# Where the last products of two unhalved tiles, one x cast and one bank copy stand in the first steps of a feed-forward

## The chip, the core and the metric

The kernel runs on one core of one Trainium2 chip. The metric is device time in microseconds of one execution, as the median of several runs. A profile of one execution gives the busy time of each engine: TensorE (PE for matmuls, PEld for weight loads), VectorE (DVE), ScalarE (ACT), GpSimd (POOL) and SyncE (SP, which here only issues DMAs).

## What is computed

A decoder trunk of two layers on 512 tokens of width 1024 in float32. Each layer is a half-step feed-forward, three token mixers side by side, and a second half-step feed-forward:

```python
def swiglu(h, w_in, w_out):
    gate, up = jnp.split(h @ w_in, 2, axis=-1)
    return (jax.nn.silu(gate) * up) @ w_out

for l in range(DEPTH):   # 2
    x = x + 0.5 * swiglu(rms_norm(x, ffn1_norm[l]), ffn1_w_in[l], ffn1_w_out[l])
    h = rms_norm(x, mix_norm[l]) @ w_mix_in[l]
    y = concatenate([short_conv(h), hgrn2(h), fox_attention(h)])   # pieces of h
    x = x + y @ w_mix_out[l]
    x = x + 0.5 * swiglu(rms_norm(x, ffn2_norm[l]), ffn2_w_in[l], ffn2_w_out[l])
```

The hidden width of a feed-forward is 2816, 22 tiles of 128 columns. The change touches the feed-forwards only, and of the four only the last three.

## The kernel before

**Numbers in two parts.** A float32 operand is split into a high part (a ScalarE cast to fp32r) and a low part (VectorE: the operand minus the high part). A product is then three matmuls, high x high (L312), high x low (L318) and low x high (L319), in `mm3`. So each operand costs ScalarE one pass and VectorE one pass before TensorE can use it.

**Tiles of a feed-forward.** The first hidden tiles, called covered (6 in the first feed-forward, 4 in the other three), are multiplied in full with the raw x while the norm is still being worked out; their banks are scaled by `self.inv` afterwards. `clear(f, i)` (L529 ff.) does this for one tile: two VectorE multiplications out of the banks into gi and ui, and a SiLU of gi on ScalarE (L266). `values(f, i)` then makes the hidden values gi * ui: two VectorE instructions of 128x256 (L673 and L670, "the last products" of that tile), written to the tiles hq. `values(0, 0)` and `values(0, 1)` belong to the first two covered tiles, (2, 0) and (2, 1) to the other two. The rest of the tiles go through `halved`, a Strassen-like scheme: a unit is a pair of hidden tiles (or of output tiles), and its product of 2x2 blocks is made with seven block products P1 to P7 instead of eight.

**A step.** `plan` writes down all steps of a feed-forward as a list. Step n is one block product of one unit, 24 matmuls of 128x256. The first unit's products come in the order P1, P2, P6, P5, P7, P3, P4 (steps 0 to 6), the next unit's P1 is step 7. In `halved` (loop at L843) a step issues, in this order: its 24 matmuls (`product`); `prepare` for the step three further on, that is, a ScalarE cast of its weights (L770) into one of three buffers hl, and later, as `rest()`, VectorE's subtraction for the low part (L772); between the two, what the product's own bank asks for; then the plan's extra work (`run(n)`: loads, sums of weight blocks, such as L758); and last the entry `self.entry[n]`, where there is one.

**Banks.** P1, P6, P7 and P4 of a unit share one PSUM bank and add to it; P2 has its own, P5 and P3 share a third. So a bank must be read before the next product writes to it: after P1 ScalarE copies it to g1 (L869); after P2 VectorE does g1 - bank (L872), and ScalarE the SiLU of it (L266); after P6 ScalarE copies the shared bank to g2 (L876); after P5 to u2 (L879); after P7 VectorE adds the shared bank to u2 (L882); after P3 to g2 (L885); after P4 the unit's hidden values are made (L673 and L670 with 128x512).

**The x of each product.** The seven products need seven sums of quarters of the normalised x. In the three later feed-forwards `enter` (from L545) makes them by hand: four quarters X (L580), then for P1, P2, P5 and P6 a high part (`high`, ScalarE, L593) and a low part (`lows[...]`, VectorE, L596 or L598) each, with additions between them (`add`, L603). Those of P7, P3 and P4 do not come before the loop of steps: they are issued at the end of steps 0 to 3, as functions in the dictionary `self.entry`, together with the last products of the covered tiles.

**What sets the order.** All these instructions of ScalarE, VectorE, POOL and SP are chained per engine by `follow` in the order in which the program issues them. So the order written in `enter`, `halved` and `self.entry` is the order on each engine, and an instruction that waits holds all behind it on that engine.

Of the kernel before, what the change touches and what calls it, by code (L numbers as in the profile page):

```python
# [13 lines left out]
AF = mybir.ActivationFunctionType  # L14
# [142 lines left out]
class Trunk:  # L157
# [381 lines left out]
    def values(self, fp, f, i, gi, ui, keep):  # L539
        V = (lambda i: self.follow("v", i)) if keep else (lambda i: i)  # L540
        a, k = divmod(f + i, 4)
        for b in range(2):
            V(self.hidden(self.quarter(fp, 0, a, b)[:, k, :], *(t[:, 256 * b : 256 * b + 256] for t in (gi, ui)), a != b))

    def enter(self, fp, w_in, then):  # L545
        nc = self.nc
        H = T // 2
        A, V = (lambda i, e=e: self.follow(e, i) for e in "av")

        def stream(f, banks, given):  # L550
            def parts(k, kk):
                r = slice(k * P, (k + kk) * P)
                return [w_in[r, f * P : (f + 2) * P], w_in[r, FF + f * P : FF + (f + 2) * P]]

            return self.stream_steps(
                [(bk, slice(c, c + P), None) for bk, c in zip(banks, (0, 256, 128, 384))],
                parts, self.xact, KD, given=given,
            )

        ba = self.next4()  # L560
        first = stream(0, ba, lambda k: k == KD - 2)
        for _ in range(4):
            next(first)
        nb = self.bank("pt" if self.ntog % 2 == 0 else "po")
        bb = self.next4()
        second = stream(2, bb, lambda k: True)
        self.ngain = self.const.tile([P, KD], F32, tag="ngain", name=self.n("ngain"))
        A(nc.scalar.activation(self.ngain, self.gain, AF.Copy, scale=-1.0))
        next(second)
        self.end_norm(nb, fp, True)  # L570
        self.table(SILU)
        next(first, None)
        next(then)
        X, self.xc, lows = {}, {}, {}

        def quarter(a, b):
            X[a, b] = t = fp.tile([P, 4, H], F32, tag=f"r{2 + 2 * a + b}", name=self.n("xn"))
            for k in range(4):
                i = 4 * a + k
                V(nc.vector.scalar_tensor_tensor(  # L580
                    out=t[:, k, :], in0=self.xT[:, i, b * H : (b + 1) * H],
                    scalar=(self.gain if a == b else self.ngain)[:, i : i + 1],
                    in1=self.inv[:, b * H : (b + 1) * H], op0=ALU.mult, op1=ALU.mult,
                ))

        def high(name):
            c = ORDER_IN.index(name)
            src, other = X[SUM[name]], name in NEGATIVE
            hi, lo = (
                fp.tile([P, 4, H], F32R, tag=f"x{w}{c}", name=self.n("xc")) for w in "hl"  # L590
            )
            self.xc[name] = hi, lo
            A(nc.scalar.activation(hi, src, AF.Copy, scale=-1.0) if other else nc.scalar.copy(hi, src))  # L593

            def low():
                V(nc.vector.scalar_tensor_tensor(  # L596
                    out=lo, in0=src, scalar=-1.0, in1=hi, op0=ALU.mult, op1=ALU.subtract
                ) if other else nc.vector.tensor_sub(lo, src, hi))  # L598

            lows[name] = low  # L600

        def add(x, y):
            V(nc.vector.tensor_add(X[x], X[x], X[y]))  # L603

        def both(name):
            high(name)
            lows[name]()

        def row():
            next(second)  # L610
            next(second, None)

        cleared = {}

        def clear(f, i):
            banks = bb if f else ba
            cleared[f, i] = self.clear(fp, banks[2 * i], banks[2 * i + 1], True)

        def values(f, i):
            self.values(fp, f, i, *cleared.pop((f, i)), True)  # L620

        quarter(0, 0)
        high("P1")
        quarter(1, 0)
        lows["P1"]()
        next(second)
        next(second)
        high("P2")
        quarter(0, 1)
        lows["P2"]()  # L630
        quarter(1, 1)
        next(second)
        next(second)
        add((0, 0), (0, 1))
        high("P5")
        clear(0, 0)
        lows["P5"]()
        next(second)
        next(second)
        next(second, None)  # L640
        add((0, 0), (1, 1))
        high("P6")
        self.given["total"]()
        lows["P6"]()
        self.given["prepare"](0)
        self.given["prepare"](1)
        clear(0, 1)
        add((0, 1), (1, 1))
        next(then)
        self.entry = {  # L650
            0: lambda: (high("P7"), values(0, 0), lows["P7"]()),
            1: lambda: (values(0, 1), high("P3")),
            2: lambda: (lows["P3"](), add((0, 0), (1, 0))),
            3: lambda: both("P4"),
            9: lambda: clear(2, 0),
            10: lambda: values(2, 0),
            12: lambda: clear(2, 1),
            13: lambda: values(2, 1),
        }
# [66 lines left out]
    def halved(self, fp, w_in, w_out, covered):  # L726
        nc = self.nc
# [3 lines left out]
        A, V, G, S = (lambda i, e=e: self.follow(e, i) for e in "avgs")  # L731
# [13 lines left out]
        def add(u, q, q2):  # L745
            G(nc.gpsimd.dma_start(raw[u, q], src(u, q2), accum_op=ALU.add))
# [70 lines left out]
        u = seq[0][:2]  # L817
# [25 lines left out]
        for n, (kind, w, p) in enumerate(seq):  # L843
# [3 lines left out]
            if p in new:  # L847
# [3 lines left out]
                u, p, acc, p in new, p in ("P2", "P3", "P4"),  # L851
                kind == "I" and p == "P1" and w in (covered, *(f0 for f0, _ in CHUNKS)),
            )
            rest = prepare(*seq[n + LEAD]) if n + LEAD < len(seq) else None
            if kind == "O":
                c, g = w

                for r, b, f in {
                    "P2": ((0, 0, -0.5),), "P1": ((0, 0, -0.5),), "P5": ((1, 1, -0.5),),
                    "P6": ((0, 1, -0.5),), "P7": ((1, 1, 0.5),), "P3": ((0, 1, 0.5),),  # L860
                    "P4": ((1, 0, 0.5),),
                }[p]:
                    xs = self.xT[:, 4 * r + 2 * g : 4 * r + 2 * g + 2, b * H : (b + 1) * H]
                    V(nc.vector.scalar_tensor_tensor(
                        out=xs, in0=pair(acc), scalar=f, in1=xs, op0=ALU.mult, op1=ALU.add
                    ))
            elif p == "P1":
                work[u, "g1"] = g1 = tmp("g1")
                A(nc.scalar.activation(g1, acc, AF.Copy, scale=-1.0))  # L869
            elif p == "P2":  # L870
                g1 = work[u, "g1"]
                V(nc.vector.tensor_sub(g1, g1, acc))  # L872
                A(self.act(g1, g1, AF.Silu))
            elif p == "P6":
                work[u, "g2"] = g2 = tmp("g2")
                A(nc.scalar.activation(g2, acc, AF.Copy, scale=-1.0))  # L876
            elif p == "P5":
                work[u, "u2"] = u2 = tmp("u2")
                A(nc.scalar.activation(u2, acc, AF.Copy, scale=-1.0))  # L879
            elif p == "P7":  # L880
                u2 = work[u, "u2"]
                V(nc.vector.tensor_add(u2, u2, acc))  # L882
            elif p == "P3":
                g2 = work[u, "g2"]
                V(nc.vector.tensor_add(g2, g2, acc))  # L885
                A(self.act(g2, g2, AF.Silu))
            else:
                g1, g2, u2 = (work[u, x] for x in ("g1", "g2", "u2"))
                c = next(i for i, (f0, nf) in enumerate(CHUNKS) if f0 <= w < f0 + nf)
                if c < 2:  # L890
                    a, k = divmod(w - CHUNKS[c][0], 4)
                    for b, g, v in ((1, g2, u2), (0, g1, acc)):
                        V(self.hidden(
                            self.quarter(fp, c, a, b)[:, k : k + 2, :], pair(g), pair(v), a != b
                        ))
                else:
                    q = (w - CHUNKS[c][0]) // 2
                    y = fp.tile([P, 2, T], F32, tag="S", name=self.n("y"), bufs=2)
                    V(nc.vector.tensor_mul(y[:, :, H:], pair(g2), pair(u2)))
                    V(nc.vector.tensor_mul(y[:, :, :H], pair(g1), pair(acc)))  # L900
                    hh, hl = (
                        fp.tile([P, 2, T], F32R, tag=f"r{t}", name=self.n("hh")) for t in tags[q]
                    )
                    self.hh.append(hh)
                    self.hl.append(hl)
# [746 lines left out]
```

## Time and profile before

| what | value |
|---|---|
| runs | 1847.47 us median of 3 (1844.77 to 1851.09) |
| the profiled execution | 1844.32 us |
| its span, first to last instruction | 1842.5 us |
| granted TensorE clock, mean over the span | 1.000 of full speed |
| instructions | 34734 |
| entries (first steps of the halved tiles) | from about 640, 967 and 1547 us |

Times inside the profile are microseconds from the start of the span. A row of the timeline gives the start, the duration, the engine, the line of the kernel, the operation with the tiles that it writes and reads, and in brackets how long the engine stood idle before it and what ended that. A row of the waits gives the engine and line that waited, what it waited for, the total in microseconds, how often, and the longest. Durations of neighbouring instructions overlap a little, so the distance from start to start says what an instruction costs its engine. Ends of matmuls are modelled, so for TensorE too the starts are the better measure.

### The profile page before, as it was taken

The numbers are of one execution on the slowest core, as the hardware profiler recorded it, in microseconds if no ns is written. First come the engines' busy times: TensorE is split into PE (matmuls) and PEld (weight loads), VectorE is DVE, ScalarE is ACT, GpSimd is POOL, SyncE is SP. The second block draws the span as 40 slices with busy tenths as digits, with TensorE's granted clock in tenths as the row PEclk, the third lists the DMA queues.
The fourth block names the chain that finished last, engine by engine and source line by source line (L and its number), as shares of the span: only waits on it lengthen the run. The fifth ranks groups of instructions, "written<-read, shape, count | busy, mean of one in ns | idle before, by whom it ended". The sixth has DMA issues, their size and how long they took to land.

```text
span 1842.5 us, 34734 instructions
## 1 busy us (share of the span) xinstructions
PE 1817.2 (99%) x14328; PEld 1686.7 (92%) x14328; DVE 1459.7 (79%) x2007; ACT 991.1 (54%) x1403; POOL 169.1 (9%) x168
## 2 busy tenths in 40 slices
PE   8999999999999999999999999999999999999999
PEld 6899999899877899999889999988997778999997
DVE  7888887676797898879678887966849878887883
ACT  4455555454676465555445555545547655555552
POOL 0011120100000001112001111201000000020210
PEclk9999999999999999999999999999999999999999
DMA  7659684233323767868265787823233237677762
GB/s 206 169 115 198 173 176 99 74 84 82 86 75 98 213 135 161 196 161 165 82 204 128 169 190 179 172 63 82 71 86 81 81 107 203 160 153 191 149 138 91
DMA packets 244782, 250.94 MB, mean 136 GB/s; under 512 B 19440, under 2 KB 229872, under 8 KB 244624
## 3 DMA queue, kind: packets, MB, share of 16 engines
q1 hardware_dynamic: 191024, 182.64, 33.0%
q0 software_dynamic: 53600, 66.09, 22.4%
q8 instruction: 112, 1.84, 0.4%
q14 instruction: 46, 0.38, 0.1%
HBM read 223.98 MB, written 2.10 MB: 123 GB/s over the span
## 4 chain that ended last, share of the span: by engine, by line
PE 87%; DVE 6%; ACT 3%; issue 2%; DMA 1%; SPq 0%; ACTq 0%
PE mm L312 13%; PE mm L319 12%; PE mm L318 12%; PE sc L312 6%; PE sc L319 6%; PE sc L318 6%; PE pt L312 6%; PE pt L318 6%; PE pt L319 6%; PE po L312 4%; PE po L318 4%; PE po L319 3%; DVE hl L302 1%; DVE hl L772 1%; PE po L1504 1%
## 5 line engine op out<-in xcount | busy, mean ns | idle before, releaser
L770 ACT CAST hl<-w 128x1024 fp32r<-128x1024 f32 x322 | 337.1, 1049 | 319.2 <-PE mm L319 77.7
L772 DVE TENSOR_TENSOR hl<-w,hl 128x1024 fp32r<-128x1024 f32 x322 | 392.6, 1221 | 92.3 <-ACT hl L770 92.0
L302 DVE TENSOR_TENSOR hl<-st,hl 128x512 fp32r<-128x512 f32 (+2 forms) x196 | 166.4, 851 | 121.0 <-ACT hl L301 119.5
L301 ACT CAST hl<-st 128x512 fp32r<-128x512 f32 (+2 forms) x196 | 146.5, 749 | 208.0 <-PE po L319 81.7
L312 PE MATMUL mm<-xc,hl 128*128 128x256 f32 (+1 forms) x732 | 201.7, 276 | 1.8 <-ACT g L876 1.4
L319 PE MATMUL mm<-xc,hl 128*128 128x256 f32 x728 | 201.4, 277 | 0.0
L318 PE MATMUL mm<-xc,hl 128*128 128x256 f32 x728 | 201.3, 277 | 0.0
L312 PE MATMUL sc<-xc,hl 128*128 128x256 f32 (+1 forms) x530 | 146.8, 278 | 2.5 <-ACT g L876 1.7
L319 PE MATMUL sc<-xc,hl 128*128 128x256 f32 x528 | 146.6, 278 | 0.0
L318 PE MATMUL sc<-xc,hl 128*128 128x256 f32 x528 | 146.4, 277 | 0.0
L312 PEld LDWEIGHTS mm<-xc,hl 128*128 128x128 f32 x732 | 137.3, 188 | 2.5 <-ACT g L876 1.8
L318 PEld LDWEIGHTS mm<-xc,hl 128*128 128x128 f32 x728 | 136.8, 188 | 0.0
L319 PEld LDWEIGHTS mm<-xc,hl 128*128 128x128 f32 x728 | 136.7, 188 | 0.1
L312 PE MATMUL pt<-xc,hl 128*128 128x256 f32 (+1 forms) x484 | 133.4, 277 | 0.0
L318 PE MATMUL pt<-xc,hl 128*128 128x256 f32 x480 | 133.2, 278 | 0.0
L319 PE MATMUL pt<-xc,hl 128*128 128x256 f32 x480 | 133.0, 277 | 0.0
L312 PE MATMUL mm<-x,hl 128*128 128x512 f32 x272 | 108.9, 401 | 0.7 <-ACT cy L1152 0.7
L319 PE MATMUL mm<-x,hl 128*128 128x512 f32 x272 | 107.6, 396 | 0.0
L318 PE MATMUL mm<-x,hl 128*128 128x512 f32 x272 | 106.7, 392 | 0.0
L312 PEld LDWEIGHTS sc<-xc,hl 128*128 128x128 f32 x530 | 99.5, 188 | 3.3 <-ACT g L876 2.1
L319 PEld LDWEIGHTS sc<-xc,hl 128*128 128x128 f32 x528 | 99.6, 189 | 0.1
L318 PEld LDWEIGHTS sc<-xc,hl 128*128 128x128 f32 x528 | 99.2, 188 | 0.0
(483 smaller groups left out, 5611.3 us busy)
## 6 DMA issues: line engine op xcount, KB each, us to landing
w<-in_ffn_w_in_dram SPq DMA_DIRECT2D x140, 512.0 KB
w<-in_ffn_w_out_dram SPq DMA_DIRECT2D x64, 512.0 KB
w<-in_ffn_w_out_dram POOLq DMA_DIRECT2D x56, 512.0 KB, 9.3
st<-in_w_mix_in_dram SPq DMA_DIRECT2D x88, 256.0 KB
st<-in_ffn_w_in_dram SPq DMA_DIRECT2D x72, 256.0 KB
w<-in_ffn_w_in_dram POOLq DMA_DIRECT2D x35, 512.0 KB, 8.3
w<-S POOLq DMA_DIRECT2D x35, 512.0 KB, 4.8
st<-in_ffn_w_out_dram SPq DMA_DIRECT2D x24, 512.0 KB
```

What stands on the lines that cost most here:

```text
L301: a = nc.scalar.copy(hi, src[:, c : c + w])
L302: b = nc.vector.tensor_sub(lo, src[:, c : c + w], hi)
L312: i = nc.tensor.matmul(acc[:, c], ah, bh[:, c], start=first and c.start == 0, stop=False, skip_group_check=True,)
L318: nc.tensor.matmul(acc, ah, bl, start=False, stop=False, skip_group_check=True)
L319: i = nc.tensor.matmul(acc, al, bh, start=False, stop=last, skip_group_check=True)
L770: A(nc.scalar.copy(hi, src))
L772: return lambda: V(nc.vector.tensor_sub(lo, src, hi))
L1504: nc.tensor.matmul(self.ob[:, t0 + u * P : t0 + 2 * P], V[:, j, h % 4].rearrange("p a d -> p (a d)"), part[:, j, u:, :].rearrange("p i t - ...
```

## The change

In `enter`, the last products of the covered tile (0, 0) move from the end of step 0 to a place ahead of the loop, and those of (0, 1) from step 1 to the end of step 7. P3's low x moves from step 2 to step 1, behind its high x, and the addition that makes P4's operand moves with it. In `halved`, for the first unit of the three feed-forwards that have an entry, ScalarE's copy of P6's bank to g2 is issued ahead of the weight cast of that step instead of behind it.

```diff
         clear(0, 1)
         add((0, 1), (1, 1))
         next(then)
+        values(0, 0)
         self.entry = {
-            0: lambda: (high("P7"), values(0, 0), lows["P7"]()),
-            1: lambda: (values(0, 1), high("P3")),
-            2: lambda: (lows["P3"](), add((0, 0), (1, 0))),
+            0: lambda: both("P7"),
+            1: lambda: (both("P3"), add((0, 0), (1, 0))),
             3: lambda: both("P4"),
+            7: lambda: values(0, 1),
             9: lambda: clear(2, 0),
...
                 kind == "I" and p == "P1" and w in (covered, *(f0 for f0, _ in CHUNKS)),
             )
+            if kind == "I" and p == "P6" and self.entry and w == covered:
+                work[u, "g2"] = g2 = tmp("g2")
+                A(nc.scalar.activation(g2, acc, AF.Copy, scale=-1.0))
             rest = prepare(*seq[n + LEAD]) if n + LEAD < len(seq) else None
...
                 A(self.act(g1, g1, AF.Silu))
+            elif p == "P6" and (u, "g2") in work:
+                pass
             elif p == "P6":
                 work[u, "g2"] = g2 = tmp("g2")
                 A(nc.scalar.activation(g2, acc, AF.Copy, scale=-1.0))
```

## The prediction, made before the changed kernel ran

> **What bounds the kernel now.** I read the page's first part, then the whole-span list of waits for TensorE, then the timeline of one entry engine by engine (634 to 690 us), and last the same stretch of the other two entries.
>
> ```profile
> PE 1817.2 (99%) x14328; PEld 1686.7 (92%) x14328; DVE 1459.7 (79%) x2007; ACT 991.1 (54%) x1403; POOL 169.1 (9%) x168
> ```
> ```profile
> PE sc L312 <- ACT g L876: 1.7, 2, 0.9
> ...
> PE mm L312 <- ACT g L876: 1.4, 2, 0.9
> ...
> PE sc L312 <- DVE u L882: 0.7, 2, 0.4
> ...
> PE mm L312 <- DVE u L882: 0.4, 1, 0.4
> ```
>
> TensorE is the bound: busy 99% of the span. So a change gains only where TensorE itself stands still. Two waits bear on this change: L876, the ScalarE copy of P6's bank into g2, and L882, the VectorE add that reads P7's bank. Entry 1 (the feed-forward at 640 us) shows where they fall. Each row below but the third is the first matmul of a product: P5, P7 (then P7's second matmul), P3, P4, and the next unit's P1 and P2.
>
> ```profile
> 648.15 0.28 PE L312 MATMUL pt<-xc,hl 128*128 128x256 f32 x1
> ...
> 651.90 0.39 PE L312 MATMUL sc<-xc,hl 128*128 128x256 f32 x1 [0.87 <-ACT g L876]
> ...
> 652.12 0.28 PE L318 MATMUL sc<-xc,hl 128*128 128x256 f32 x1
> ...
> 654.74 0.28 PE L312 MATMUL pt<-xc,hl 128*128 128x256 f32 x1
> ...
> 657.98 0.36 PE L312 MATMUL sc<-xc,hl 128*128 128x256 f32 x1 [0.36 <-DVE u L882]
> ...
> 660.80 0.28 PE L312 MATMUL pt<-xc,hl 128*128 128x256 f32 x1
> ...
> 663.52 0.28 PE L312 MATMUL sc<-xc,hl 128*128 128x256 f32 x1
> ```
>
> An undisturbed product takes 663.52 - 660.80 = 2.72 us for its 24 matmuls. The four from P5 on took 3.75, 2.84, 3.24 and 2.82. Their excess is 1.03 + 0.12 + 0.52 + 0.10 = **1.77 us** per entry: more than the 0.87 + 0.36 that the waits name, because the idle counts begin at a modelled matmul end, and because the first matmul after each stall goes slower (652.12 - 651.90 = 0.22, where 2.72/24 is 0.113). The other two entries show the same two stalls:
>
> ```profile
> 979.13 0.39 PE L312 MATMUL mm<-xc,hl 128*128 128x256 f32 x1 [0.87 <-ACT g L876]
> ...
> 985.22 0.36 PE L312 MATMUL mm<-xc,hl 128*128 128x256 f32 x1 [0.36 <-DVE u L882]
> ```
> ```profile
> 1558.80 0.39 PE L312 MATMUL sc<-xc,hl 128*128 128x256 f32 x1 [0.86 <-ACT g L876]
> ...
> 1564.88 0.36 PE L312 MATMUL sc<-xc,hl 128*128 128x256 f32 x1 [0.36 <-DVE u L882]
> ```
>
> So the most that can come from this is 3 x 1.77 = **5.3 us**, 0.29% of the span; about 0.3% is what a measurement of this kernel can tell from no change.
>
> The Trainium skill, "TensorE: Matmul & The Clock Gate", Part 1, "Wait — 56ns, not 53.3ns?", gives a warm matmul N / 2.4 GHz plus some 2.5 ns. An estimate from that page is 109 ns at N = 256, or 2.62 us per product, so an excess of 12.65 - 4 x 2.62 = 2.17 us per entry and 6.5 us in all. The trace differs: undisturbed products beside the stalls take 2.72 us, so the 5.3 stands.
>
> **Why TensorE waits there.** ScalarE and VectorE in that stretch of entry 1, in their order:
>
> ```profile
> 648.84 0.64 ACT L266 ACTIVATE g<-g 128x512 f32<-128x512 f32 x1 [1.27 <-DVE g L872]
> 649.38 1.03 ACT L593 CAST xc<-xn 128x1024 fp32r<-128x1024 f32 x1
> 650.32 1.04 ACT L770 CAST hl<-w 128x1024 fp32r<-128x1024 f32 x1
> 651.26 0.58 ACT L876 ACTIVATE g<-sc 128x512 f32<-128x512 f32 x1
> 651.75 1.04 ACT L770 CAST hl<-w 128x1024 fp32r<-128x1024 f32 x1
> ...
> 654.92 1.06 ACT L593 ACTIVATE xc<-xn 128x1024 fp32r<-128x1024 f32 x1 [1.63 <-DVE xn L603]
> ```
> ```profile
> 646.32 0.42 DVE L673 TENSOR_TENSOR hq<-gi,ui 128x256 f32<-128x256 f32 x1
> 646.65 0.42 DVE L670 SCALAR_TENSOR_TENSOR hq<-gi,ui 128x256 f32<-128x256 f32 x1
> 646.99 1.22 DVE L596 SCALAR_TENSOR_TENSOR xc<-xn,xc 128x1024 fp32r<-128x1024 f32 x1
> 648.12 0.68 DVE L872 TENSOR_TENSOR g<-g,sc 128x512 f32<-128x512 f32 x1
> 648.72 1.22 DVE L772 TENSOR_TENSOR hl<-w,hl 128x1024 fp32r<-128x1024 f32 x1
> 649.86 0.42 DVE L673 TENSOR_TENSOR hq<-gi,ui 128x256 f32<-128x256 f32 x1
> ...
> 651.39 1.22 DVE L772 TENSOR_TENSOR hl<-w,hl 128x1024 fp32r<-128x1024 f32 x1 [0.78 <-ACT hl L770]
> 652.53 1.22 DVE L598 TENSOR_TENSOR xc<-xn,xc 128x1024 fp32r<-128x1024 f32 x1
> 653.66 1.22 DVE L603 TENSOR_TENSOR xn<-xn,xn 128x1024 f32<-128x1024 f32 x1
> 654.80 1.22 DVE L772 TENSOR_TENSOR hl<-w,hl 128x1024 fp32r<-128x1024 f32 x1
> 656.01 1.23 DVE L596 SCALAR_TENSOR_TENSOR xc<-xn,xc 128x1024 fp32r<-128x1024 f32 x1
> 657.16 0.68 DVE L882 TENSOR_TENSOR u<-u,sc 128x512 f32<-128x512 f32 x1
> ```
>
> VectorE's add at 648.12 reads P2's bank, free since P6 began at 648.15 - 2.72 = 645.43, so it comes 2.7 us late, held by VectorE's own list. ScalarE's SiLU waits for it, then come P3's x, a weight cast, and only then P6's copy, which ends at 651.84; P7 starts 0.06 later. The add for P7's bank stands at the end of an unbroken VectorE run from 651.39, ends at 657.84, and P4 starts 0.14 later.
>
> **The change, part by part.** In each entry three things move on VectorE and one on ScalarE; the order of TensorE, POOL and SP is the same, and so is every DMA issue. No instruction is added or removed.
>
> 1. The pair (0,0) of last products, two VectorE instructions costing 646.99 - 646.32 = 0.67 us, goes ahead of the loop: in front of the low half of the third weight product. That slot is free, as VectorE next stands idle for 1.62 us (row at 644.04 below). The low half ended at 644.04 - 1.62 = 642.42, now 643.1 at the latest, and is first needed by P6 at 645.43, so the price is nothing; without that idle it would be 0.67 per entry. From 646.32 on VectorE runs 0.67 earlier: P7's low x ends at 647.5, the add L872 starts at 647.45, the SiLU at 648.17, P3's high x at 648.71.
> 2. P6's copy passes one cast, worth 650.32 -> 651.26 = 0.94 us. It starts at 648.71 + 0.94 = 649.65 and ends at 650.24 (P6's product is complete: P5 began at 648.15). P7's turn is 648.15 + 2.72 = 650.87: the copy is 0.6 ahead, and the **first stall goes**. The passed cast starts at 650.14, after 650.32 before, so it does not get later; its weight tile comes by a POOL transfer issued at 638.9 that landed within 6.5 us (rows below).
> 3. The pair (0,1) leaves VectorE's list ahead of the casts' subtractions, and P3's low x and the following add move ahead of the subtraction for P3's weights. P3's low x can start when ScalarE has its high half, 648.71 + 1.03 + 0.03 = 649.77; behind it, at 1.14 to 1.2 each as in the rows from 651.39, come the add (650.9), the two subtractions (652.05, 653.2), P4's low x (654.4) and the add L882 (655.55 to 656.23). This is 1.6 earlier than 657.16. ScalarE's share, P4's high x, waits for the add: in the row at 654.92 it starts 0.04 after the add's 653.66 + 1.22; now it may from 652.2 on, behind a cast and a bank copy, and is done ahead of 654.4. P4 can start at 656.23 + 0.14 = 656.37; its turn is 648.15 + 3 x 2.72 = 656.31. So the **second stall shrinks to about 0.06**, with perhaps 0.1 for a slower first matmul.
> 4. New wait: P3 now waits by itself for its weights' low half, which ends at 653.3; the matmul that reads it is due at 653.59 + 0.23. Cover 0.5 us, price nothing; if it failed, P3 and all behind it would be late by the shortfall.
> 5. The pair (0,1) is added at step 7, ahead of the next unit's L872 add. Behind that wait the SiLU, a cast and the next copy. VectorE's idle there:
>
> ```profile
> 644.04 1.23 DVE L772 TENSOR_TENSOR hl<-w,hl 128x1024 fp32r<-128x1024 f32 x1 [1.62 <-ACT hl L770]
> ...
> 668.41 1.23 DVE L772 TENSOR_TENSOR hl<-w,hl 128x1024 fp32r<-128x1024 f32 x1 [0.60 <-ACT hl L770]
> 670.29 1.23 DVE L772 TENSOR_TENSOR hl<-w,hl 128x1024 fp32r<-128x1024 f32 x1 [0.66 <-ACT hl L770]
> ```
> ```profile
> L787 POOL DMA_DIRECT2D w<-S x1: 887/887/887, 638.9 to 638.9; - x1
> ...
> DMA to landing us min/median/max: 6.5/6.5/6.5
> ```
> ```profile
> 670.16 0.59 ACT L876 ACTIVATE g<-pt 128x512 f32<-128x512 f32 x1
> ```
>
> The 0.67 is nearly all taken by the 0.60 of idle right behind, and the copy of the next unit ended at 670.75, 0.9 before its P7 at 660.80 + 4 x 2.72 = 671.68. Price nothing; uncovered, at most 0.67 per entry.
>
> **Sum.** Entries 1 and 3 gain 1.77 - 0.15 = 1.6 each; entry 2, whose second stall has the same size, 1.6 to 1.77. Together 5.0 us, between 0 (nothing reaches the end) and 5.3. Nearer 5.3 than 0, since the list of waits names no TensorE wait in later halved steps of these three feed-forwards (the rest of the 1.4 above belongs to the first one, which the change leaves alone). The profiled run took 1844.32 us, 1.8 more than its span of 1842.5, and goes to 1839.3. The median of the three runs shown is 1847.47, 3.15 above the profiled run; from it the forecast is **1842.4**.
>
> **Rivals.**
> - *The second stall stays in part.* If ScalarE's SiLU chain comes d later than worked out, P4 waits d longer, since VectorE's five following instructions have no gap. With d = 0.8, about the idle 0.78 that VectorE had at 651.39, an entry gains 1.6 - 0.8 = 0.8, together 2.4: 1845.1. For it: only 0.06 separates P4's turn from the add. Against it: the order of ScalarE ahead of that point is unchanged.
> - *VectorE is the limit, or a transfer takes the gain back.* Nothing is removed, so work that only moves gives nothing where VectorE has no idle: 1847.5. The Trainium skill, "VectorE: DVE Perf Modes", section "Rules for kernel authors", says to cut the number of instructions, since each pays its flush however they are chained; by it the moved pairs cost the same wherever they stand. Against it: the idle of 1.62, 0.60 and 0.66 us above. For the transfers: weights loaded long before would not come earlier with TensorE.
> - *The pair at step 7 costs more than it frees.* The next unit's L872 comes 0.67 late, its copy passes the 0.9 of slack, and P7 of that unit stalls as the first unit's did, at 1.15 us (1.03 + 0.12), while L882 of the first unit keeps its old time and P4's start with it. Then nothing is gained and 3 x 1.15 = 3.5 is lost: 1851.0, slower. It decides once VectorE's queue at step 8 is over 0.9 us later against TensorE than in these rows; the idle rows speak against it.
>
> **How the numbers follow.** Forecast 0.75, second stall in part 0.12, swallowed 0.08, slower 0.05. The bound of 0.3% is 5.5 us, so faster means under 1841.9. The three runs of before lie 6.3 us apart, so a median near 1842.4 falls on either side: I give the forecast 0.5 faster, 0.48 same, 0.02 slower; the partial case 0.15, 0.8, 0.05; the swallowed one 0.05, 0.8, 0.15; the last 0, 0.3, 0.7. Faster 0.40, same 0.54, slower 0.06. The range goes from the 5.3 with the lower runs' scatter (1838) to the swallowed gain (1847).
>
> **What would show it.** Right: in the profile after, the list of waits has no TensorE wait for the g2 copy at the three entries and at most a trace of L882, four products from P5 on take 10.9 to 11.1 us instead of 12.65, and P6's copy ends before 650.9 by this clock. Wrong: a new TensorE wait at P3 (its low half), or at the next unit's P7; or the stalls gone while the span is unchanged, which would mean that a transfer or a later stage took it.

## The result

| | before | after |
|---|---|---|
| median of 7 runs, us | 1845.43 (1841.21 to 1851.09) | 1838.22 (1835.24 to 1839.66) |
| ratio | | 0.9961, 95% interval 0.9945 to 0.9977 |
| profiled execution, us | 1844.32 | 1837.37 |
| its span, us | 1842.5 | 1835.6 |

The changed kernel is 0.39% faster, 7.2 us by the medians. The forecast from the median of three runs was 1842.4, that is, 5.0 us less; the time lies inside the range by 0.2 us. Two more measurements of the same two kernels gave 0.9966 (0.9952 to 0.9979) and 0.9971 (0.9955 to 0.9987).

First the list of TensorE's waits over the whole span of the profile after (engine, line, what it waited for, total, times, longest), from its third row to the row for the copy:

```profile
PE pt L1551 <- DVE KB L1473: 1.6, 6, 0.3
PE pt L1245 <- issue: 1.4, 1, 1.4
PE sc L1307 <- issue: 1.3, 2, 0.7
PE po L312 <- DVE nt L399: 1.3, 1, 1.3
PE mm L312 <- ACT cy L1158: 0.8, 2, 0.4
PE po L1510 <- ACT PH L1553: 0.6, 2, 0.3
PE mm L312 <- ACT g L882: 0.5, 1, 0.5
```

L882 is the old place of P6's copy in the new numbering; its one wait of 0.5 belongs to the first feed-forward. The copy's other waits are gone: neither its new place (L857) nor the add for P7's bank (now L888) has a row in the list. The same products as before, P5, P7, P3, P4, then the next unit's P1 and P2, in the timeline of entry 1:

```profile
647.90 0.28 PE L312 MATMUL pt<-xc,hl 128*128 128x256 f32 x1
...
650.62 0.28 PE L312 MATMUL sc<-xc,hl 128*128 128x256 f32 x1
...
653.34 0.28 PE L312 MATMUL pt<-xc,hl 128*128 128x256 f32 x1
...
656.07 0.33 PE L312 MATMUL sc<-xc,hl 128*128 128x256 f32 x1
...
658.83 0.28 PE L312 MATMUL pt<-xc,hl 128*128 128x256 f32 x1
...
661.55 0.28 PE L312 MATMUL sc<-xc,hl 128*128 128x256 f32 x1
```

They take 2.72, 2.72, 2.73 and 2.76: 10.93 in place of 12.65. What is left of the two stalls is 0.05 us. ScalarE and VectorE in that stretch of the same timeline:

```profile
647.91 0.63 ACT L266 ACTIVATE g<-g 128x512 f32<-128x512 f32 x1 [0.60 <-DVE g L876]
648.45 1.04 ACT L593 CAST xc<-xn 128x1024 fp32r<-128x1024 f32 x1
649.40 0.58 ACT L857 ACTIVATE g<-sc 128x512 f32<-128x512 f32 x1
649.88 2.04 ACT L771 CAST hl<-w 128x1024 fp32r<-128x1024 f32 x2
```
```profile
647.20 0.68 DVE L876 TENSOR_TENSOR g<-g,sc 128x512 f32<-128x512 f32 x1
647.80 1.22 DVE L773 TENSOR_TENSOR hl<-w,hl 128x1024 fp32r<-128x1024 f32 x1
649.53 1.23 DVE L598 TENSOR_TENSOR xc<-xn,xc 128x1024 fp32r<-128x1024 f32 x1 [0.51 <-ACT xc L593]
650.67 1.22 DVE L603 TENSOR_TENSOR xn<-xn,xn 128x1024 f32<-128x1024 f32 x1
651.80 2.35 DVE L773 TENSOR_TENSOR hl<-w,hl 128x1024 fp32r<-128x1024 f32 x2
654.07 1.22 DVE L596 SCALAR_TENSOR_TENSOR xc<-xn,xc 128x1024 fp32r<-128x1024 f32 x1
655.21 0.68 DVE L888 TENSOR_TENSOR u<-u,sc 128x512 f32<-128x512 f32 x1
```

This execution reached the entry 0.25 us earlier than the one of before (first product at 639.61; in before at 639.86). With that taken off, the prediction's times are met almost to the hundredth: the copy (L857) ends at 649.98 where 649.99 was worked out, P3's low x (L598) starts at 649.53 for 649.52, the add L888 ends at 655.89 for 655.98, and P4 starts at 656.07 for 656.12.

**Where the 6.9 us between the two spans came from.** I cut both spans at points that both have: the norms (the first matmul of L405), and the products whose first matmul is split in two (the first of each chunk of hidden tiles; in the timeline a row with 128x128 and x2). The differences, after minus before, in order:

| stretch | before, us | after, us | difference |
|---|---|---|---|
| start of the span to entry 1 | | | -0.25 |
| entry 1 to the next chunk | 40.0 | 38.3 | -1.7 |
| the chunk behind it | 114.5 | 118.9 | +4.4 |
| entry 2 to the next chunk | 40.8 | 39.1 | -1.7 |
| mixer of layer 2, norm to norm | 259.8 | 258.2 | -1.6 |
| entry 3 to the next chunk | 40.0 | 38.3 | -1.7 |
| the chunk behind it | 118.9 | 114.6 | -4.3 |
| the rest | | | -0.1 |

The three entries give 5.1 (the expectations below have it as 5.2). The two chunks trade places: one of them takes 118.9 us for the same matmuls in either profile, the second feed-forward's in one, the fourth's in the other. The mixer of layer 2, which no instruction of the change touches, gave 1.6. So theory A says: the change gains the 5.1 of the entries, and the rest is scatter of single executions. Theory B: it also took something away outside the entries. A second question is how the parts act together: each its own share, or in series.

### The profile page after: what moved, and what is told of

Same layout as the page of the kernel before. It is cut to its first block, busy times and chain, and to the rows that moved or that the text cites. A ratio compares the mean times of both kernels' runs of the same rounds, so it can differ in the third digit from the quotient of the medians.

```text
span 1835.6 us, 34734 instructions
## 1 busy us (share of the span) xinstructions
PE 1815.1 (99%) x14328; PEld 1685.2 (92%) x14328; DVE 1459.1 (79%) x2007; ACT 991.8 (54%) x1403; POOL 169.1 (9%) x168
## 4 chain that ended last, share of the span: by engine, by line
PE 89%; DVE 5%; ACT 3%; issue 1%; DMA 1%; SPq 1%; ACTq 0%
PE mm L312 13%; PE mm L319 13%; PE mm L318 13%; PE sc L319 6%; PE sc L318 6%; PE sc L312 6%; PE pt L312 6%; PE pt L318 6%; PE pt L319 6%; PE po L312 4%; PE po L318 4%; PE po L319 4%; DVE hl L302 1%; PE po L1510 1%; ACT hl L301 1%
```

## The experiments

All ratios are against the kernel before, run on the same chip in the same series; the comparisons of one series share its runs of before. The ratios differ from the quotients of the two medians by up to 0.0008, which is 1.5 us.

### The same two kernels again

No edit.

> The kernel before, once more, against itself. Both theories: ratio 1.000 with an interval of some 0.002 each way. Theory A (the change gains what the two stalls cost, 5.2 us, and the other 1.7 us of the difference of the two profiled spans, 6.9, is scatter): the excess of the four products from P5 on over 4 x 2.72 us is again about 1.77 us in entries 1 and 3, and places other than the entries differ from the first profile of before by a microsecond or more, among them the stretches of some 100 us in which a product takes 2.83 instead of 2.72 us. Theory B (the change also took something away outside the entries): outside the entries this profile agrees with the first one of before to a few tenths.

> The changed kernel once more. Theory A: 5.2 us less than before, ratio 0.9972; the excess of the four products from P5 on is below 0.1 us in each entry; the layer-2 mixer, where the first profile of after was 1.5 us shorter than that of before, is not shorter by the same amount again. Theory B: ratio 0.9961 or less again, and the mixer again 1.5 us shorter.

> The changed kernel a third time, on another day's scatter. Theory A (the gain is what the stalls cost): 5.2 us less than before, ratio 0.9972, entries of 38.3 us (39.1 where the slow pace sets in). Rival (the change also keeps TensorE out of slow stretches): ratio 0.9964 or less again.

Before against itself: 0.9999 (0.9987 to 1.0011). After: 0.9966 (0.9952 to 0.9979), and 0.9971 (0.9955 to 0.9987) the third time. Entries to the next chunk, in us: before 40.0, 40.8, 40.8; after 39.1, 39.1, 38.3 and 38.3, 38.3, 38.3. An entry that has 0.8 more than its kernel's shortest has it as slow pace, not as a wait: its products behind P4 take 2.83 instead of 2.72. In the first entry of the second profile of after that pace begins with P4 itself, so the excess there is 0.16 and not below 0.1, as was expected. The mixer of layer 2 took 261.2 in the repeat of before, and 260.2 and 262.8 in those of after, 258.2 to 262.8 in all profiles, with the longest of them in the changed kernel. So theory B's loss there did not come back. The ratios of after, 0.9961 to 0.9971, agree with theory A's 0.9972, each interval holding it; but all three lie below it, and a gain of some microseconds more (by the lower ends up to 3), everywhere and evenly, they cannot exclude.

### The copy alone

```diff
+            if kind == "I" and p == "P6" and self.entry and w == covered:
+                work[u, "g2"] = g2 = tmp("g2")
+                A(nc.scalar.activation(g2, acc, AF.Copy, scale=-1.0))
             rest = prepare(*seq[n + LEAD]) if n + LEAD < len(seq) else None
```
(against the kernel before; self.entry as there. The branch for P6 further down then passes, as in the change.)

> Only P6's bank copy ahead of the cast; the entries as before. Theory A: the first stall nearly goes (copy ends at 650.9 by the clock of before, P7 due 650.87), but the cast behind the copy comes 0.49 us later, and with it VectorE's unbroken run up to the add for P7's bank, so P4 starts at about 658.5 instead of 657.98: 0.5 us more per entry, 1.5 us slower in all, ratio 1.0008. Rival (each part gives its own share of the gain, the copy the first stall of 1.15 us): 3.4 us faster, ratio 0.998.

Measured 0.9995 (0.9986 to 1.0005). The timeline of entry 1 (which began 2.5 us later in this execution; P5 at 650.66), with P7, P3, P3's second matmul, P4 and the next unit's P1, then VectorE's add:

```profile
653.46 0.39 PE L312 MATMUL sc<-xc,hl 128*128 128x256 f32 x1
...
656.39 0.28 PE L312 MATMUL pt<-xc,hl 128*128 128x256 f32 x1
656.79 0.39 PE L318 MATMUL pt<-xc,hl 128*128 128x256 f32 x1
...
660.97 0.36 PE L312 MATMUL sc<-xc,hl 128*128 128x256 f32 x1 [1.28 <-ACT hl L770]
...
663.78 0.28 PE L312 MATMUL pt<-xc,hl 128*128 128x256 f32 x1
```
```profile
654.37 1.23 DVE L772 TENSOR_TENSOR hl<-w,hl 128x1024 fp32r<-128x1024 f32 x1 [1.26 <-ACT hl L770]
...
660.14 0.68 DVE L887 TENSOR_TENSOR u<-u,sc 128x512 f32<-128x512 f32 x1
```

The first stall shrinks from 1.03 to 0.08 (653.46 - 650.66 = 2.80). A new one comes at P3, whose second matmul starts 0.40 behind its first instead of 0.11. P4 starts 10.31 us after P5 instead of 9.83: the 0.5 worked out, and the four products take 13.12 in place of 12.65. So the copy alone makes the entry worse, by 0.47: VectorE's subtraction waits 1.26 (0.78 before) for the cast that was passed, and its unbroken run ends 0.47 later. The rival of shares asked for 3.4 us off, ratio 0.998; the profile refutes it, and the interval does not reach so low. The time does not show the 1.4 us: its interval ends at 1.0005, a little under the 1.0008 expected. And one lesson in reading: the row at 660.97 blames a ScalarE cast, yet P4 needs no cast that late; the add that it does need ended at 660.14 + 0.68 = 660.82, 0.15 ahead of it, as 0.14 before the change.

### The moves in the entries alone

```diff
+        values(0, 0)
         self.entry = {
-            0: lambda: (high("P7"), values(0, 0), lows["P7"]()),
-            1: lambda: (values(0, 1), high("P3")),
-            2: lambda: (lows["P3"](), add((0, 0), (1, 0))),
+            0: lambda: both("P7"),
+            1: lambda: (both("P3"), add((0, 0), (1, 0))),
             3: lambda: both("P4"),
+            7: lambda: values(0, 1),
```
(against the kernel before; the copy behind the cast as there)

> Only the moves in the entries; P6's copy stays behind the cast. Theory A: ScalarE runs 0.67 us earlier, the copy ends at about 651.2 by the clock of before, P7 is late by 0.35 and some 0.1 for its slow first matmul; P4 does not wait. An entry gains 1.77 - 0.45 = 1.3, together 3.9 us, ratio 0.9979. Rival (shares that add up: the copy the first stall, the entry moves the second): 1.9 us faster, ratio 0.999, with P7 still late by 0.8 or more.

> The entry moves without the copy, once more: its first runs lay 5.9 us under before, where its stalls in the profile account for 3.9. Theory A with scatter: 3.9 us, ratio 0.9979, entries of 38.7, 38.7 to 39.8 and 38.7 us. Rival (the entry moves also keep TensorE out of the stretches in which a product takes 2.83 us): again 6 us or more, ratio 0.9967 or less, and no stretch of 118.9 us between two chunks.

Measured 0.9962 (0.9949 to 0.9976) and 0.9983 (0.9962 to 1.0004). In the timeline of entry 1, P6's copy, and P7, which was due 2.72 after P5 at 648.38:

```profile
650.83 0.58 ACT L877 ACTIVATE g<-sc 128x512 f32<-128x512 f32 x1
```
```profile
651.46 0.39 PE L312 MATMUL sc<-xc,hl 128*128 128x256 f32 x1 [0.20 <-ACT g L877]
```

P7 is late by 0.36 and P4 not at all; the four products take 659.75 - 648.38 = 11.37. That is 1.28 off an entry, as expected; 38.7 us to the next chunk. The first series measured more than the 3.8 us that this makes, the second about that, and the second's profile has a chunk of 118.9 us: the moves do not keep the slow pace away.

### The first pair alone, and with the copy

```diff
+        values(0, 0)
         self.entry = {
-            0: lambda: (high("P7"), values(0, 0), lows["P7"]()),
+            0: lambda: both("P7"),
             1: lambda: (values(0, 1), high("P3")),
```
(against the kernel before; second kernel: this and the copy ahead of the cast)

> Only the pair (0,0) goes ahead of the loop; the pair (0,1) stays ahead of P3's subtraction, P3's low x stays at step 2, the copy stays behind the cast. Theory A: ScalarE runs 0.67 us earlier, so P7 is late by 0.35 and 0.1 for its slow first matmul; VectorE's unbroken run starts 0.67 earlier, so P4 starts at 657.3 by the clock of before instead of 657.98. Each entry gains 0.66, from the entry's first product to the next chunk's 39.3 us instead of 40.0; 2.0 us in all, ratio 0.9989. Rival (shares add up): nothing at P4, since the run there still has its pair: 0.4 at P7 only.

> The pair (0,0) ahead of the loop and P6's copy ahead of the cast; pair (0,1) and P3's low x as before. Theory A: P7 no longer waits at all, yet the cast behind the copy and VectorE's run behind it are 0.49 later than in pair_alone, so P4 starts at 657.8 and the entry gains only 0.17 (39.8 us instead of 40.0): 0.5 us in all, ratio 0.9997, worse than pair_alone by 1.5 us though one of the two stalls is gone. Rival (shares add up): the first stall's 1.15 and the pair's share, over 3.4 us, ratio under 0.9982.

Measured 0.9985 (0.9963 to 1.0008) and 0.9976 (0.9956 to 0.9997). With the first pair alone both stalls shrink; P7 (due at 649.68 + 2.72 = 652.40) and P4:

```profile
652.76 0.38 PE L312 MATMUL sc<-xc,hl 128*128 128x256 f32 x1 [0.20 <-ACT g L877]
...
658.84 0.36 PE L312 MATMUL sc<-xc,hl 128*128 128x256 f32 x1 [0.35 <-DVE u L883]
```

P4 comes 658.84 - 649.68 = 9.16 after P5, 0.67 earlier than before's 9.83. With the copy added P7 waits for nothing, and P4, with P5 at 649.30:

```profile
658.95 0.36 PE L312 MATMUL sc<-xc,hl 128*128 128x256 f32 x1 [1.29 <-ACT hl L771]
```

9.65 after P5, worse by 0.49 than without the copy, all as worked out. Neither interval tells these sizes apart (2.0 and 0.5 us); the starts in the profile do. The second kernel's 0.9976 taken by itself would even suit the rival of shares (under 0.9982); what speaks against the rival is P4, which comes later with the copy than without it. The entries of the second kernel take 40.6 us, not 39.8: all three go on at the slow pace behind P4, which was not expected.

### More work at step 7

Against the changed kernel:

```diff
-            7: lambda: values(0, 1),
+            7: lambda: [self.values(fp, 0, 1, *cleared[0, 1], True) for _ in range(3)] + [values(0, 1)],
```

> The changed kernel with the pair (0,1) computed four times at step 7 instead of once (the three extra ones write the same values again): 2.0 us more on VectorE ahead of the next unit's add for g1. By the profile of after (copy of that unit's P6 ended at 668.78, its P7 due at 669.71) the copy comes 1.9 late, P7 is late by 0.95 and 0.1 for its slow first matmul: 39.4 us from the entry's first product to the next chunk's instead of 38.3, together 3.2 us slower than after, ratio to before 0.9989. If the slack at step 7 were much smaller than the 0.9 us of the prediction, up to 2.0 per entry: 6 us slower than after; if larger, the same as after.

Measured 0.9996 (0.9976 to 1.0017), which holds the expected 0.9989 and the same time as before alike; the profile has entries of 40.1 us each. The next unit's P7 and P3:

```profile
671.38 0.38 PE L312 MATMUL pt<-xc,hl 128*128 128x256 f32 x1 [0.80 <-ACT g L882]
...
674.84 0.38 PE L312 MATMUL sc<-xc,hl 128*128 128x256 f32 x1 [0.46 <-ACT u L885]
```

P7 came 671.38 - 667.70 = 3.68 after P5 instead of 2.72: late by 0.96 for the 0.95 expected, so the slack of 0.9 at step 7 was right, and the pair that the change puts there costs nothing. What I had not seen is the second stall: ScalarE's copy of P5's bank stands behind the late ones and holds P3 by another 0.6. An entry loses 1.8 instead of 1.1, all that the change had gained.

### The copy in the first feed-forward too

Against the changed kernel:

```diff
-            if kind == "I" and p == "P6" and self.entry and w == covered:
+            if kind == "I" and p == "P6" and w == covered:
```

> The changed kernel with P6's copy ahead of the cast in the first feed-forward too, where it has no entry and where, by the profile of after, P7 still waits for it (0.82 us from one matmul to the next at 94.79, so 0.81 lost with the slow first matmul). Theory A: that stall goes, but the passed cast and what VectorE does behind it come up to 0.5 later, so the add for P7's bank ends at 99.7 to 100.1 and P4, due at 99.53, waits: 0.0 to 0.4 us gained out of 0.8. Rival (the stall named is the gain): 0.8 us gained. Neither shows in the time, only in the profile; ratio to before 0.997 as after.

Measured 0.9962 (0.9943 to 0.9981). P7's wait there is gone, and P4, in the timeline, waits:

```profile
99.66 0.38 PE L312 MATMUL mm<-xc,hl 128*128 128x256 f32 x1 [0.20 <-DVE u L888]
```

The stretch from the first halved product to the next split one takes 19.65 us instead of 20.0: 0.35 of the 0.8 that the stall cost. By the stalls this version is 0.35 ahead of the changed kernel, which no measurement here can tell from none.

## Why the prediction was right, and where it was off

- **What bounds the kernel, and 1.77 us an entry.** Right. In the profiles the time from P5's start to the next unit's P1 tells the state of an entry: 12.65 before, 13.12 with the copy alone, 11.37 with the moves alone, 10.93 with both.
- **Part 1, the pair (0,0).** Right; everything behind came 0.67 earlier, shown alone by pair_alone.
- **Part 2, the copy.** Right in the whole change: it ends 0.6 ahead of P7's turn. But the first stall's price is not the copy's gain. Alone the copy costs 0.5 an entry, on top of the moves it gains 0.44 (11.37 to 10.93).
- **Part 3, the second stall.** Right: 0.05 us is left of both, where 0.15 was allowed. The sum is 1.72 + 1.7 + 1.72 = 5.1, for the 5.0 of the forecast.
- **Part 4, the new wait at P3.** No cost: P3's subtraction ended at 653.02 (651.80 and the 1.22 of one such row) and TensorE did not pause.
- **Part 5, the pair at step 7.** Nothing, as forecast, and its 0.9 of slack was measured by the fourfold pair. The slower rival needed more than that; in its price it left out that a second bank copy is held as well.
- **The rivals.** The partial case did not occur (add done at 655.89, P4 at 656.07); VectorE had the idle that the moved work needed.
- **The number.** 1842.4 against 1838.22 is 4.2 us. Of this, 2.0 is the base of the sum, the term that was off: the median of three runs, 1847.47, was 2.0 above the one of seven, 1845.43. Another 0.1 is the entries' 5.1 for 5.0. The last 2.1 is what this series shows beyond 5.1; in the two later series it was 1.1 and 0.2 by the ratios, 0.3 and -1.0 by the medians. So it was luck that the time stayed inside the range by 0.2 us, and that the change came out over 0.3%, for which the chance was put at 0.40, was a matter of that scatter; by the profile it is 0.28%.
- **The 2.62 us per product** that the prediction estimated from the Trainium skill ("TensorE: Matmul & The Clock Gate", Part 1, "Wait — 56ns, not 53.3ns?") was met nowhere: undisturbed products take 2.72, slow ones 2.83.

What stays open: by the ratios nine of the ten comparisons of changed kernels came out faster than their stalls account for, by 1.5 us on the average of all ten; for two, the copy alone and the first series of the moves, the account lies just outside the interval. By the medians it is seven of ten, and 0.7 us. The profiles show no place for it: with the slow pace of the last section taken off, the spans of after lie no further below those of before than the entries explain. That is a handful of single executions, so a small gain elsewhere is not excluded.

## What to carry to other kernels

When a busy engine stalls twice in a row, find the queue that both stalls hang on: here VectorE's list set ScalarE's SiLU, which set the first stall, and ended in the second. Removing the first stall alone only moved the wait, and made it longer, because the instruction passed was needed by the second. Work out the due times of all instructions behind a moved one, and count stalls from start to start of the work, not by the idle time that is named.

## What the runs showed of the hardware that was not expected

TensorE runs the same matmuls at two paces. A chunk of 42 steps takes 114.4 to 114.6 us or 118.9, with nothing between; products take 2.72 or 2.83 us. The windows view of the profile after, the same chunk in the second and the fourth feed-forward (busy time and count of each engine, granted clock, DMA share, GB/s):

```profile
677.90:796.80 118.90, 118.90 (x1011) 118.78 (x1010) 98.00 (x103) 61.76 (x70) 16.53 (x14) 1.00 0.72 169
1584.20:1698.80 114.60, 114.60 (x1012) 114.49 (x1011) 97.57 (x103) 61.77 (x70) 16.53 (x14) 1.00 0.74 175
```

TensorE has the same work and is busy throughout, and the granted clock is 1.00 in both. In the twelve profiles 9 of the 36 such chunks of the three later feed-forwards were slow, 2 of 6 with before, 4 of 12 with the changed kernel and its extension, so I see no tie to the change.

A slow stretch began at a break in TensorE's work, however small. In the slow chunk above the second product came late. Judging by the times, it waited for VectorE's L671, which reads its bank and ends at 679.99 + 0.69 = 680.68, 0.15 ahead of it; the last matmul of the first product and the first of the second:

```profile
679.99 0.69 DVE L671 SCALAR_TENSOR_TENSOR hq<-g,pt 128x512 f32<-128x512 f32 x1
```
```profile
680.61 0.28 PE L319 MATMUL pt<-xc,hl 128*128 128x256 f32 x1
680.83 0.36 PE L312 MATMUL pt<-xc,hl 128*128 128x256 f32 x1
```

The distance is 0.22 where 0.113 is usual, and from there on the pace is slow. This break stands in 23 of the 36 chunks: 9 of them went on slowly, 14 did not (114.6 us). The 13 chunks without it were all quick (114.4). These 13 follow the 13 entries that themselves ended at the slow pace and so were 0.8 to 1.1 us longer, and in each of those the slow pace set in at its last stall, P4's, or P7's with the moves alone. Even the 0.05 that the change leaves at P4 can be enough: in 5 of the 12 entries of the changed kernel and its extension the slow pace followed it, which cost more than the stall itself. A slow stretch ended at a stall, with the feed-forward, or within 2 us of the next product whose first matmul is split in two. All this was seen in the timelines, not tried, and why one break is followed by the slow pace and another is not stays open.

Counted over all matmuls of 128x256 in a span, the slow pace (4.5 ns more for each) cost from 1.8 us, with more work at step 7, to 12.8 us, in the third profile of after. With it taken off, the spans of after are 1829.5, 1832.2 and 1833.3 and those of before 1835.0 and 1837.9: 4.8 us apart on the average, beside the 5.1 of the entries. So one execution can lose or win more by its pace than this change gains.
